# Moving the state-space output products one turn later, and fourteen matmuls on a tile of ones at the start

## The chip, the core and the metric

The kernel runs on one core of a Trainium2 chip. A core has a matmul engine (TensorE, "PE" in the profile, its weight loads "PEld"), a vector engine (VectorE, "DVE"), a scalar engine (ScalarE, "ACT"), a general engine (GpSimd, "POOL") and a queue that issues transfers (SyncE, "SP"). Each engine takes its instructions in the order of the program, and waits for others by semaphores. The metric is the time of one execution in microseconds of the device. Before the change it is 2964.65 us, the median of 3 runs (2963.62 to 2970.11).

## The reference

Two layers over 256 positions of width 4096. Layer 0 has a state-space mixer (S5), layer 1 a gated linear recurrence; both attend to a fixed memory. What matters here is the mixer of layer 0, cut from the reference:

```python
proj = rmsnorm(h, pre_norm[i]) @ w_in[i]
u, gate, q, q_gate = split(proj)                 # u: 3072 wide, 192 groups of 16 channels
ab = exp(lam * dt)                               # complex, 64 states to a group
x  = einsum('blgc,gpc->lbgp', u, bb)             # input products
s  = associative_scan(x with decay ab)           # complex states
y  = einsum(s_re, c_re) - einsum(s_im, c_im)     # output products
y  = y + d_skip * u
g  = gelu(y)
out = g * sigmoid(g @ w_glu + b_glu)
```

After it `out * silu(gate)` and the attention's part go through one output projection, and the normalised result is added to `h`.

## The kernel before

All matmuls with large weights run in *steps*. A step takes a block of 512 KB of weights (`raw`), which SP loads five steps ahead. ACT casts it to a rounded copy `hi` and DVE subtracts to get the rest `lo` (`split_w`, two steps ahead); TensorE then multiplies both parts (`mm_step`). There are three buffers for `raw` and six halves each for `hi` and `lo`, so the cast for step i + 2 waits for the matmuls of step i - 1, and the load for step i + 5 waits for the split of step i + 2.

The program is written out by `run`, one turn for each step: first what is due in that turn (`at(k, f)` puts a piece of work into turn k, and pieces of one turn run in the order in which they were put there), then the step's matmuls, the split of a later step, side work, and the load of a still later one. So the turn in which a piece stands sets its place in the queue of every engine that it uses.

The mixer is cut into 24 row groups `ct` of 128 channels. When the scan is done, `s5` gives each group a start turn S = S0 + 3·ct and puts its pieces into turns around it (`y_tasks`, lines 908 to 947):

- S - 9, S - 5, S - 2: SP loads the output coefficients as given (`s["craw"]`, tensor `in_s5c`), `b2` and `u`.
- S - 7: `y_coef`. POOL works out four sets of output coefficients, for the four positions of a block of time: per set two products over 128 x 128 (lines 883 and 884, into `P` and `Q`) and four sums over 64 x 64 (lines 887 and 888), 24 instructions in all. They go into `Cs[ct % 3]`: **three buffers in turn**, so group ct + 3 is written where group ct was.
- S: `d_mm`, 8 small matmuls into `psd`, which read sets 0 to 2 of that buffer.
- S + 1: `d_copy`, four copies by ACT from `psd` into `aux`.
- S + 2: `y_mm`, the output products. Three matmuls read `aux` and `u`, then 32 small ones read the states and the buffer `Cs[ct % 3]`, in the order set 1, set 2, set 3, set 0. All write one half of the PSUM tile `pm`.
- S + 3 to S + 8: skip term on DVE (`f3`), GELU on ACT and DVE, and the store of the result (`f8`, tensor `gF`).

While this runs, the steps are those of `gq0`, `q0` and the first of `k0`; at the same time the memory is normalised (`st` from `in_mem`) for `k0`. Three steps and one group's `d_mm` and `y_mm` make one period on TensorE.

At the very start SP loads the first weight block and the first parts of `x`; ACT makes the first operand `A` from them, and then TensorE has its first matmul.

Of the kernel before, what the change touches and what calls it, by code (L numbers as in the profile page):

```python
# [14 lines left out]
AF = mybir.ActivationFunctionType  # L15
# [13 lines left out]
L4 = 4  # L29
TQ = T // L4  # L30
MAGIC = 12582912.0

SM = {}
_o = 0
# [28 lines left out]
class Trunk:  # L63
# [77 lines left out]
    def at(self, k, fn):  # L141
        self.due.setdefault(max(k, self.step + self.late), deque()).append(fn)
# [6 lines left out]
    def setup(self):  # L149
        tc, ctx = self.tc, self.ctx  # L150
        P = lambda name, bufs, **kw: ctx.enter_context(tc.tile_pool(name=name, bufs=bufs, **kw))
        self.cpool = P("const", 1)
        self.wraw = P("wraw", 3)
        self.whi = P("whi", 6)
        self.wlo = P("wlo", 6)
        self.big = P("big", 1)
        self.ev = P("ev", 3)
        self.stp = P("st", 2)
        self.ps_acc = P("psacc", 4, space=PSUM)
        self.ps_x = P("psx", 3, space=PSUM)  # L160
        self.ps_m = P("psm", 1, space=PSUM)
        self.pm = self.ps_m.tile([128, 2, T], F32, name="pm")
        self.dram = P("dram", 1, space=DRAM)
        dt = lambda n, s, d=F32: self.dram.tile(s, d, name=n, tag=n)
        self.uF = dt("uF", [KE, 128, T])
        self.aD = dt("aD", [NT, 2, 2, 64])
        self.wD = dt("wD", [KE, 2, L4, 16, 512])
        self.uX = dt("uX", [KE, 2, L4, 64, 64])
        self.gF = dt("gF", [KE, 128, T])
        self.sil = dt("sil", [KE, 128, T])  # L170
        self.hs = dt("hs", [KE, 128, T])
        self.og = dt("og", [KD, 128, T])
        self.h1 = dt("h1", [KD, 128, T])
        self.qd = [dt(f"qd{i}", [KX, 128, T]) for i in range(2)]
        self.sq = [dt(f"sqd{i}", [KX, 128, T]) for i in range(2)]
        self.kd = [dt(f"kd{i}", [KX, 128, T]) for i in range(2)]
        self.vd = [dt(f"vd{i}", [2, 128, XA]) for i in range(2)]
        c = self.cpool
        self.sm = c.tile([128, SM_W], F32, name="sm")
        self.ones = c.tile([128, 128], F32, name="ones")  # L180
        self.ident = c.tile([128, 128], F32, name="ident")
        self.n4sp = c.tile([128, KE], F32, name="n4sp")
        self.acc = c.tile([128, 2, T], F32, name="acc")
        self.rbx = c.tile([128, T], F32, name="rbx")
        self.rbm = c.tile([128, T], F32, name="rbm")
        self.colm = c.tile([128, 2], F32, name="colm")
        self.nc.vector.memset(self.ones, 1.0)
        make_identity(self.nc, self.ident)

    def small(self, name, i, n=1):  # L190
        o = SM[name][0] + i
        return self.sm[:, o:o + n]
# [473 lines left out]
    def exp_gen(self, y, x, t):  # L666

        k, r, p, z, ki = t
        self.ts(y, x, -104.0, ALU.max, 88.0, ALU.min)
        self.ts(k, y, 1.4426950408889634, ALU.mult, MAGIC, ALU.add)  # L670
        self.ts(k, k, MAGIC, ALU.subtract)
        yield
# [19 lines left out]
    def sincos_gen(self, s, c, th, t):  # L692
        k, r, z, q, m1, m2 = t
        self.ts(k, th, 0.6366197723675814, ALU.mult, MAGIC, ALU.add)
        self.ts(k, k, MAGIC, ALU.subtract)
        yield
# [7 lines left out]
        self.ts(c, z, 2.443315711809948e-5, ALU.mult, -1.388731625493765e-3, ALU.add)  # L704
        self.ts(q, q, MAGIC, ALU.add)
        self.mul(s, s, z)
        self.mul(c, c, z)
        yield
        self.ts(q, q, MAGIC, ALU.subtract)
        self.ts(s, s, -1.6666654611e-1, ALU.add)  # L710
# [38 lines left out]
    def s5(self):  # L749
        I, at = self.I, self.at  # L750
# [112 lines left out]
        def y_load(ct, part):  # L863
            s = st.setdefault(ct, {})
            if part == 0:
                s["craw"] = v4(tail(1536 + 128 * (ct % 2), 128))
                self.dma(s["craw"], I["s5c"][ct])
            elif part == 1:
                s["b2"] = v4(tail(1792 + 256 * (ct % 2), 256))
                self.dma(s["b2"], I["s5b2"][ct])  # L870
            else:
                s["u"] = sp.tile([128, T], F32, name="u", tag="u")
                for i in range(4):
                    self.dma(s["u"][32 * i:32 * i + 32], self.uF[ct].rearrange("(q i) t -> i q t", i=4)[i])

        def y_coef(ct):
            s = st[ct]
            P, Q = v4(tail(2304, 128)), v4(tail(2432, 128))
            g = self.nc.gpsimd
            for i, (re, im) in enumerate(kc):  # L880
                C = Cs[ct % 3][:, i]
                b = lambda v: v[:, 4 * ct:4 * ct + 4].unsqueeze(1).unsqueeze(3).to_broadcast([128, 2, 4, 16])
                g.tensor_tensor(out=P, in0=s["craw"], in1=b(re), op=ALU.mult)
                g.tensor_tensor(out=Q, in0=s["craw"], in1=b(im), op=ALU.mult)
                for h in range(2):
                    r, c = slice(64 * h, 64 * h + 64), slice(16 * h, 16 * h + 16)
                    g.tensor_tensor(out=C[r, 0, :, c], in0=P[r, 0], in1=Q[r, 1], op=ALU.add)
                    g.tensor_tensor(out=C[r, 1, :, c], in0=Q[r, 0], in1=P[r, 1], op=ALU.subtract)

        def d_mm(ct):  # L890
            s = st[ct]
            s["d"] = self.ps_x.tile([128, 3, 32], F32, name="psd", tag="x")
            for k in range(2):
                for j in range(4):
                    self.mm(s["d"][32 * j:32 * j + 32], s["b2"][:, k, j, :], Cs[ct % 3][:, 0:3, k, j, :],
                            k == 0, k == 1, 66)

        def d_copy(ct):
            d = D[ct % 2]
            for j in range(4):  # L900
                r = slice(32 * j, 32 * j + 32)
                self.acopy(d[r, :, r], st[ct]["d"][r])

        def y_mm(ct):
            s = st[ct]
            ps = self.pm[:, 1, :].rearrange("p (e t) -> p e t", e=L4)
            s["y"] = ps
            C, d, u = Cs[ct % 3], D[ct % 2], s["u"].rearrange("p (e t) -> p e t", e=L4)
            for i in range(3):
                self.mm(ps[:, i:3, :], d[:, i, :], u[:, 0:3 - i, :], i == 0, False, 330 - 53 * i)  # L910
            for e in range(L4):
                o = e == L4 - 1
                for k in range(2):
                    for j in range(4):
                        self.mm(ps[32 * j:32 * j + 32, e, :], C[:, 0 if o else e + 1, k, j, :],
                                X[:, ct * 4 + j, k, o:o + TQ], o and k == 0, e > 1 and k == 1, 60)

        def y_tasks(ct, S):
            s = st.setdefault(ct, {})
            y = tail(256 * (ct % 4), 256)  # L920
            w = tail(1024 + 256 * (ct % 2), 256)

            def f3():
                self.stt(y.rearrange("p (t e) -> p e t", e=L4), s["u"].rearrange("p (e t) -> p e t", e=L4),
                         self.small("d", ct), s["y"], ALU.mult, ALU.add)

            def f4():
                self.act(w, y, AF.Square)
                self.act(w, w, AF.Identity, scale=0.044715, bias=self.ones[:, 0:1])

            def f8():
                self.dma(self.gF[ct], y)
                self.done.add(("g", ct))
                del st[ct]
            at(S - 9, lambda: y_load(ct, 0))
            at(S - 5, lambda: y_load(ct, 1))
            at(S - 7, lambda: y_coef(ct))
            at(S - 2, lambda: y_load(ct, 2))
            at(S, lambda: d_mm(ct))
            at(S + 1, lambda: d_copy(ct))  # L940
            at(S + 2, lambda: y_mm(ct))
            at(S + 3, f3)
            at(S + 4, f4)
            at(S + 5, lambda: self.mul(w, w, y))
            at(S + 6, lambda: self.act(w, w, AF.Sigmoid, scale=1.5957691216057308))
            at(S + 7, lambda: self.mul(y, y, w))
            at(S + 8, f8)

        a = z = 0
        last = -9  # L950
# [24 lines left out]
        S = self.step + 10  # L975
        for ct in range(KE):
            y_tasks(ct, S + 3 * ct)
# [440 lines left out]
```

## Time and profile before

| what | value |
|---|---|
| median of 3 runs | 2964.65 us |
| the profiled execution, its own time | 2964.16 us |
| its span in the profile | 2962.4 us |
| TensorE busy | 2894.9 us, 98% of the span |
| DVE, ACT, POOL busy | 1969.3, 1598.3, 303.7 us |
| from the first `d_mm` to the last | 643.61 to 917.73 us |
| POOL's coefficients, first start to last | 625.34 to 915.03 us |

A busy TensorE means that some matmul is under way, so idle time is what can be removed or added directly, and its clock is the other thing to look at: the profile has a column for the clock that was granted, 1.00 being the full 2.4 GHz and 0.50 the lower 1.2 GHz. In the stretch of the output products POOL is busy nearly all the time; elsewhere it has little to do.

### The profile page before, as it was taken

How to read it: one execution, taken by the hardware profiler on the slowest of the kernel's cores; microseconds unless marked ns; L12 is line 12 of the kernel's file. 1: busy time of each engine (PE TensorE's matmuls, PEld its weight loads, DVE VectorE, ACT ScalarE, POOL GpSimd, SP SyncE). 2: the span in 40 equal slices, each digit the busy share in tenths (PEclk: the TensorE clock that was granted, in tenths of full speed). 3: DMA queues.
4: the chain of work that ended last, by engine and by line, in shares of the span. 5: the costliest groups of instructions: out<-in, count | busy, mean ns of one | idle time of the engine just before them, and what ended most of it. 6: DMA issues, size and time to landing. Idle time of an engine off the chain costs nothing.

```text
span 2962.4 us, 53046 instructions
## 1 busy us (share of the span) xinstructions
PE 2894.9 (98%) x19182; PEld 2537.9 (86%) x19182; DVE 1969.3 (66%) x3559; ACT 1598.3 (54%) x3042; POOL 303.7 (10%) x607
## 2 busy tenths in 40 slices
PE   8989999999989999999999999999999999999996
PEld 8978888888879898888888888888888888888885
DVE  8776459976586556666555776578788766655555
ACT  6334554445465556566555564466666655555553
POOL 0000000059993000000000110000000000000001
PEclk9999999999999999999999999999999999999998
DMA  7688756665566676677666896666667575666664
GB/s 247 203 248 264 228 197 188 193 203 188 185 219 199 220 246 228 218 232 231 196 208 202 267 307 199 200 205 212 210 209 224 195 235 189 201 201 201 203 203 155
DMA packets 279319, 633.64 MB, mean 214 GB/s; under 512 B 42464, under 2 KB 149216, under 8 KB 279008
## 3 DMA queue, kind: packets, MB, share of 16 engines
q1 hardware_dynamic: 272848, 624.22, 66.5%
q0 software_dynamic: 4352, 4.20, 0.9%
q8 instruction: 150, 2.46, 0.3%
q10 hardware_dynamic: 1856, 1.84, 0.2%
q14 instruction: 113, 0.93, 0.1%
HBM read 585.47 MB, written 46.24 MB: 213 GB/s over the span
## 4 chain that ended last, share of the span: by engine, by line
PE 87%; DVE 5%; DMA 4%; issue 2%; ACT 1%; SPq 1%; POOL 0%; DVEq 0%; ACTq 0%
PE acc L131 83%; DVE lo L91 2%; PE pm L131 2%; DMA raw<-in_w_q 1%; PE psg L131 1%; DMA raw<-in_w_u 1%; DVE Bs L91 1%; PE psx L131 1%; ACT hi L127 1%; DVE e L91 1%; DMA st<-in_mem 1%; SPq L135 1%; DVE Bfin L91 0%; PE pso L131 0%; PE pss L131 0%
## 5 line engine op out<-in xcount | busy, mean ns | idle before, releaser
L91 DVE TENSOR_TENSOR lo<-raw,hi 128x512 fp32r<-128x512 f32 x1960 | 1315.6, 696 | 885.1 <-ACT hi L127 847.1
L127 ACT CAST hi<-raw 128x512 fp32r<-128x512 f32 x1960 | 1153.7, 619 | 818.1 <-PE acc L131 425.3
L131 PE MATMUL acc<-A,hi 128*128 128x512 f32 (+1 forms) x4768 | 1483.4, 370 | 22.0 <-ACT hi L127 13.7
L131 PE MATMUL acc<-A,lo 128*128 128x256 f32 x4160 | 1169.5, 281 | 4.6 <-DVE lo L91 4.4
L131 PEld LDWEIGHTS acc<-A,hi 128*128 128x128 f32 x4768 | 861.6, 190 | 185.0 <-ACT hi L127 16.5
L131 PEld LDWEIGHTS acc<-A,lo 128*128 128x128 f32 x4160 | 789.9, 190 | 11.4 <-DVE lo L91 10.3
L131 PE MATMUL acc<-Bhn,hi 128*128 128x512 f32 x2048 | 719.4, 396 | 3.3 <-ACT hi L127 3.3
L131 PE MATMUL acc<-Bhn,lo 128*128 128x256 f32 x2048 | 572.9, 280 | 1.3 <-DVE lo L91 1.3
L131 PEld LDWEIGHTS acc<-Bhn,hi 128*128 128x128 f32 x2048 | 384.8, 188 | 93.1 <-ACT hi L127 4.3
L131 PEld LDWEIGHTS acc<-Bhn,lo 128*128 128x128 f32 x2048 | 386.8, 189 | 2.9 <-DVE lo L91 2.6
L131 PE MATMUL acc<-Bmix,hi 128*128 128x512 f32 x1024 | 355.0, 394 | 0.0
L131 PE MATMUL acc<-Bmix,lo 128*128 128x256 f32 x1024 | 283.6, 277 | 0.0
L131 PEld LDWEIGHTS acc<-Bmix,hi 128*128 128x128 f32 x1024 | 192.0, 188 | 44.7
L131 PEld LDWEIGHTS acc<-Bmix,lo 128*128 128x128 f32 x1024 | 192.1, 188 | 0.0
L131 PE MATMUL acc<-hi,A 128*128 128x512 f32 x512 | 157.7, 389 | 0.0
L649 POOL TENSOR_TENSOR Bfin<-Bfin 128x1024 f32<-128x1024 f32 x4 | 10.3, 2586 | 1186.8 <-DVE Bfin L91 1186.8
L127 ACT COPY e<-acc 128x256 f32<-128x256 f32 x212 | 78.1, 368 | 90.2 <-PE acc L131 89.1
L131 PEld LDWEIGHTS acc<-hi,A 128*128 128x128 f32 x512 | 95.8, 188 | 19.7
L578 POOL DMA_DIRECT2D bh<-in_x x16 | 19.3, 1208 | 823.2 <-ACT hi L127 759.7
L123 ACT ACTIVATE e<-e 128x256 f32<-128x256 f32 x64 | 26.8, 418 | 139.7 <-DVE e L91 139.5
L131 PE MATMUL acc<-lo,A 128*128 128x512 f32 x256 | 99.6, 389 | 0.0
L91 DVE TENSOR_TENSOR e<-e,acc 128x256 f32<-128x256 f32 x212 | 84.4, 410 | 7.1 <-ACT e L127 7.1
(151 smaller groups left out, 1789.2 us busy)
## 6 DMA issues: line engine op xcount, KB each, us to landing
raw<-in_w_out SPq DMA_DIRECT2D x256, 512.0 KB, 4.2
raw<-in_w_u SPq DMA_DIRECT2D x192, 512.0 KB, 4.4
raw<-in_w_g SPq DMA_DIRECT2D x192, 512.0 KB, 4.0
raw<-in_w_glu SPq DMA_DIRECT2D x72, 512.0 KB, 4.2
raw<-in_w_gq SPq DMA_DIRECT2D x64, 512.0 KB, 4.4
raw<-in_w_q SPq DMA_DIRECT2D x64, 512.0 KB, 4.3
raw<-in_w_k SPq DMA_DIRECT2D x64, 512.0 KB, 4.5
raw<-in_w_v SPq DMA_DIRECT2D x64, 512.0 KB, 4.3
```

What stands on the lines that cost most here:

```text
L91: self.nc.vector.tensor_tensor(out=out, in0=a, in1=b, op=op)
L123: self.nc.scalar.activation(out=out, in_=a, func=f, **kw)
L127: self.nc.scalar.copy(out=out, in_=a)
L131: self.nc.tensor.matmul(out, lhsT=lhsT, rhs=rhs, start=start, stop=stop)
L135: self.nc.sync.dma_start(out=out, in_=in_)
L578: self.nc.gpsimd.dma_start(out=h, in_=self.I["x"][2 * c:2 * c + 2].rearrange("k p t -> p k t"), accum_op=ALU.add)
L649: self.nc.gpsimd.tensor_tensor(out=o, in0=o, in1=h, op=ALU.add)
```

## The change

```diff
+NWARM = 14
@@ setup
         make_identity(self.nc, self.ident)
+        for _ in range(NWARM):
+            self.nc.tensor.matmul(self.pm[:, 0, 0:128], lhsT=self.ones, rhs=self.ones, start=True, stop=True)
@@ y_tasks
             at(S, lambda: d_mm(ct))
             at(S + 1, lambda: d_copy(ct))
-            at(S + 2, lambda: y_mm(ct))
-            at(S + 3, f3)
-            at(S + 4, f4)
-            at(S + 5, lambda: self.mul(w, w, y))
-            at(S + 6, lambda: self.act(w, w, AF.Sigmoid, scale=1.5957691216057308))
-            at(S + 7, lambda: self.mul(y, y, w))
-            at(S + 8, f8)
+            at(S + 3, lambda: y_mm(ct))
+            at(S + 4, f3)
+            at(S + 5, f4)
+            at(S + 6, lambda: self.mul(w, w, y))
+            at(S + 7, lambda: self.act(w, w, AF.Sigmoid, scale=1.5957691216057308))
+            at(S + 8, lambda: self.mul(y, y, w))
+            at(S + 9, f8)
```

`y_mm` and all that follows it stand one turn later; the loads, `y_coef`, `d_mm` and `d_copy` stay. `y_mm(ct)` is now in the turn of `d_mm(ct + 1)` and ahead of it. `y_coef(ct + 3)` stands in turn S + 2 of group ct. It was behind `y_mm(ct)` in that turn; now it is one turn ahead of it, with the same buffer. So in the program's order the products of groups 0 to 20 read what `y_coef(ct + 3)` has written.

The first place is TensorE's queue at the first output products, group 0. `C_3035` is the first coefficient buffer, `Bs_370` the large tile with the states, and what stands in brackets are the engines or transfers that the row waits for. Before:

```order
L131 MATMUL acc<-A,lo 128x256
L131 MATMUL pm<-u,aux 128x192 [waits DMAHW6_49,DMAHW1_49,DMAHW7_49,DMAHW0_49,Activation_49]
L131 MATMUL pm<-u,aux 128x128
L131 MATMUL pm<-u,aux 128x64
L131 MATMUL pm<-Bs_370,C_3035 32x64 x16
L131 MATMUL pm<-Bs_370,C_3035 32x64 [waits Pool_49]
L131 MATMUL pm<-Bs_370,C_3035 32x64 x3
L131 MATMUL pm<-Bs_370,C_3035 32x64 [waits Pool_49]
L131 MATMUL pm<-Bs_370,C_3035 32x64 x11
L131 MATMUL acc<-A,hi 128x512
```

The two waits for POOL stand at set 3, the last that POOL writes for this group; sets 0 to 2 were already waited for by `d_mm`. The same place after the change (the lines of the file are one higher, and the buffers have other numbers: `C_3049` is the first coefficient buffer, `C_3050` the second):

```order
L132 MATMUL pm<-u,aux 128x64
L132 MATMUL pm<-Bs_384,C_3049 32x64 [waits Pool_49]
L132 MATMUL pm<-Bs_384,C_3049 32x64 x3
...
L132 MATMUL pm<-Bs_384,C_3049 32x64 [waits Pool_49]
L132 MATMUL pm<-Bs_384,C_3049 32x64 x11
L132 MATMUL psd<-C_3050,Bs_384 32x96 [waits DMAHW2_49]
```

Now each of the two halves (real and imaginary) of sets 1, 2 and 3 has a wait for POOL of its own, six in all, of which the first and the last are shown; `d_mm` of the next group, the row with `psd`, stands behind them and has none.

The second place is SP's queue in the middle of this stretch. `gF<-Bs` is the store of a finished group, `Bs<-in_s5c` the load of raw coefficients for a group six later. Before:

```order
L135 DMA raw<-in_w_q 128x1024
L135 DMA gF<-Bs_370 128x256
L135 DMA raw<-in_w_q 128x1024
L135 DMA Bs_370<-in_s5c 128x128
L135 DMA raw<-in_w_q 128x1024
L135 DMA u<-uF 32x256 x4
```

After:

```order
L136 DMA raw<-in_w_q 128x1024 x2
L136 DMA gF<-Bs_384 128x256
L136 DMA Bs_384<-in_s5c 128x128
L136 DMA raw<-in_w_q 128x1024
L136 DMA u<-uF 32x256 x4
```

The store went past one load of weights and now stands directly ahead of the load of raw coefficients. The queue of POOL is the same row for row before and after.

## Rows read from the trace of the kernel before

**Rows 1.** The page, part 1: busy time, share and instructions by engine.
```profile
PE 2894.9 (98%) x19182; PEld 2537.9 (86%) x19182; DVE 1969.3 (66%) x3559; ACT 1598.3 (54%) x3042; POOL 303.7 (10%) x607
```

**Rows 2.** Sum over the stretches of the 24 groups, 625.34 to 915.36.
```profile
sum 290.02, PE 279.48 PEld 243.66 DVE 195.27 ACT 165.88 POOL 269.44; mean PE 27.95 PEld 24.37 DVE 19.53 ACT 16.59 POOL 26.94
```

**Rows 3.** Waits of PE, 620 to 930: total us, times, longest.
```profile
PE pm L131 <- ACT aux L127: 10.5, 7, 3.3
```

**Rows 4.** Waits of ACT, 640 to 930, the largest.
```profile
ACT hi L127 <- DMA raw<-in_w_q: 44.8, 21, 5.7
```

**Rows 5.** Waits of SP's queue, 640 to 930, the largest.
```profile
SPq L135 <- POOL Bs L884: 113.3, 21, 7.3
```

**Rows 6.** Timeline of POOL: start us, length us, engine, line, instruction.
```profile
625.34 0.40 POOL L883 TENSOR_TENSOR Bs<-Bs,cf 128x128 f32<-128x128 f32 x1 [5.07 <-DMA Bs<-in_s5c]
...
651.63 0.40 POOL L883 TENSOR_TENSOR Bs<-Bs,cf 128x128 f32<-128x128 f32 x1
...
652.47 0.32 POOL L887 TENSOR_TENSOR Bs<-Bs 64x64 f32<-64x64 f32 x1
...
653.80 0.40 POOL L883 TENSOR_TENSOR Bs<-Bs,cf 128x128 f32<-128x128 f32 x1
...
656.78 0.40 POOL L883 TENSOR_TENSOR Bs<-Bs,cf 128x128 f32<-128x128 f32 x1
...
673.87 0.73 POOL L883 TENSOR_TENSOR Bs<-Bs,cf 128x128 f32<-128x128 f32 x1
...
915.03 0.33 POOL L888 TENSOR_TENSOR Bs<-Bs 64x64 f32<-64x64 f32 x1
```

**Rows 7.** Timeline of PE at the small matmuls of the mixer.
```profile
643.61 0.54 PE L131 MATMUL psd<-C,Bs 128*32 128x96 f32 x16
...
649.83 0.88 PE L131 MATMUL pm<-u,aux 128*128 128x192 f32 x6
650.64 1.11 PE L131 MATMUL pm<-Bs,C 128*32 128x64 f32 x64
...
654.70 0.54 PE L131 MATMUL psd<-C,Bs 128*32 128x96 f32 x16
...
772.57 0.98 PE L131 MATMUL pm<-u,aux 128*128 128x192 f32 x6 [0.83 <-ACT aux L127]
...
831.95 0.98 PE L131 MATMUL pm<-u,aux 128*128 128x192 f32 x6 [2.16 <-ACT aux L127]
...
917.73 0.54 PE L131 MATMUL psd<-Bs 128*32 128x96 f32 x16
```

**Rows 8.** Stretches: length, busy PE, PEld, DVE, ACT, POOL; clock, DMA, GB/s.
```profile
774.00:776.00 2.00, 2.00 (x52) 1.73 (x41) 2.00 (x4) 1.46 (x3) 1.92 (x4) 1.00 0.00 0
...
834.00:836.00 2.00, 2.00 (x25) 1.64 (x17) 0.93 (x3) 1.02 (x3) 1.86 (x5) 0.50 0.13 41
```

**Rows 9.** Transfers by kind: instructions, KB, median us to landing.
```profile
Bs<-in_s5c SPq DMA_DIRECT2D x24, 64.0 KB, 1.8
```

**Rows 10.** Timeline of the start.
```profile
0.84 0.17 DVE L187 MEMSET ones<- 128x128 f32 x1 [0.84 <-PEq L1400]
...
8.04 0.58 PE L131 MATMUL acc<-A,hi 128*128 128x256 f32 x1 [8.04 <-ACT A L123]
...
13.05 0.41 PE L131 MATMUL acc<-A,lo 128*128 128x256 f32 x1
...
13.69 0.41 PE L131 MATMUL acc<-A,lo 128*128 128x256 f32 x1
...
14.57 0.28 PE L131 MATMUL acc<-A,lo 128*128 128x256 f32 x1
...
14.93 0.28 PE L131 MATMUL acc<-A,lo 128*128 128x256 f32 x1
```

**Rows 11.** The start by stretch, columns as in Rows 8.
```profile
10.00:12.00 2.00, 2.00 (x12) 2.00 (x11) 2.00 (x5) 2.00 (x5) 0.00 (x0) 1.00 0.83 306
```

**Rows 12.** Matmuls on the tile of ones: ns min/median/max.
```profile
L131 PE MATMUL pm<-dg,ones x20: 270/275/580, 89.7 to 2940.4; 128*128 128x128 f32 x20
```

## The prediction

> **What bounds the kernel now.** I read the page's part 1 first: TensorE has work under way in 2894.9 us, 98% of the span [rows 1], so whatever moves TensorE's queue moves the end. Then I went to the stretch that the change touches, the 24 groups of output products, by stretches: from the first coefficient to the last POOL is busy 269.4 of 290.0 us, its gaps being those between its instructions, while TensorE with 279.5 still has idle time, and DVE with 195.3 and ACT with 165.9 are far from full [rows 2]. POOL's timeline gives its pace: group 0 starts at 625.34, group 4 at 673.87, and the last of group 23 ends at 915.03 + 0.33 = 915.36 [rows 6]; that is 241.5 us for the 20 groups from 4 on, 12.07 each. TensorE left alone needs less: from d_mm to d_mm, 643.61 to 654.70, are 11.09 us [rows 7]. In these, y_mm takes 649.83 to 650.64 + 1.11 = 651.75, that is 1.92, d_mm 0.54, and each of three steps (11.09 - 1.92 - 0.54) / 3 = 2.88. So POOL is the slower of the two, and TensorE ends the stretch on POOL's heels: its last d_mm starts at 917.73 [rows 7], 2.4 us behind POOL's last coefficient.
>
> The waits say how this shows. TensorE waits for `aux`, the copies, 10.5 us in 7 places [rows 3]. But the copies are late because ACT's queue stands at casts that wait 44.8 us for weights [rows 4], and the weights are late because SP's queue stands 113.3 us at the reload of raw coefficients, whose place POOL has not read yet [rows 5]. The end of that chain is POOL's pace.
>
> **The change, part by part.** *The turn between copy and product.* It takes away the reason that the trace names, up to 10.5 us. I count it at nothing: POOL runs through without a wait before, so a TensorE that comes sooner only meets it elsewhere.
>
> *The buffer.* This is what decides. Three buffers go in turn, and y_mm(ct) now stands behind y_coef(ct + 3), which writes its buffer; it reads what that wrote, and waits for it. Before, it needed POOL's group ct; now POOL must be three groups further.
>
> First stop: TensorE reaches y_mm(0) one step later than before, at 649.83 + 2.88 = 652.7. POOL's group 3 ended at 673.87 (the start of group 4) [rows 6]. While TensorE stands, the splits stop and DVE runs dry; POOL has a quicker pace when DVE leaves it alone: one set took 653.80 - 651.63 = 2.17 us, four make 8.7, against 12.07 on the mean [rows 6]. With two sets of group 2 left at 656.78, group 3 is complete at 656.78 + 2 x 2.17 + 8.7 = 669.8; I take 670. The ends are this and 673.9. TensorE stands about 17 us.
>
> The Trainium skill (SBUF — State Buffer, § Who interferes with whom) says that a DVE instruction with two SBUF inputs and a GpSimd instruction that reads SBUF exclude each other for a whole instruction; that is a mechanism for the two paces. By it the early end, 670, holds; without it the sum below would be 4 us larger. That the first set of group 2 took 2.17 us and the second 656.78 - 653.80 = 2.98 [rows 6] agrees with it.
>
> After that the two engines are tied. POOL's last write of group ct + 3 releases the rest of y_mm(ct): 12 of its 32 small matmuls, 12/32 of 1.11 us = 0.42; then d_mm(ct + 1), 0.54; only then may POOL write group ct + 4 where d_mm(ct + 1) has read. POOL meanwhile does the first two products, 652.47 - 651.63 = 0.84 us [rows 6, 7]. With some 0.2 us for each of the two signals (an estimate: y_mm's first small matmul follows its first three by less, but on one engine) TensorE's side is 1.36, so POOL loses about 0.5 us a group, 10 us over the 20 groups. Bounds: nothing, if the signals are quick, and 1.2 each, 24 us, if the raw coefficients come late too. They are loaded three turns before use, now behind a store that SP issues just ahead; SP gets there some 10 us into a period of 12.6, and the load lands in 1.8 [rows 9], so they just fit.
>
> POOL's own 12.07 a group I leave as they are: the same instructions beside the same DVE work. Then its last group ends at 670 + 241.5 + 10 = 921.5, against 915.36.
>
> The rest: before, TensorE had only d_mm(23) left to start at that point. Now it has y_mm(20)'s rest, and from d_mm(21) to d_mm(23) two periods. 921.5 + 0.2 + 0.42 + 2 x 11.09 = 944.3, against 917.73: **26.5 us later**. Both kernels have the same work behind that point, so nothing gives it back. All that follows y_mm, one turn later on DVE, ACT and SP, I put at nothing: these engines are covered by TensorE's standing.
>
> *The burst.* Fourteen matmuls of ones can start when DVE has written the tile, 0.84 + 0.17 = 1.01, and the first real matmul waits for ACT until 8.04 [rows 10]. That one's step has 24 matmuls. Three of them take 13.69 - 13.05 = 0.64 us, soon after 14.93 - 14.57 = 0.36 [rows 10]: if all ran at the second pace, 8 x 0.28 = 2.2 us are won. The stretch view gives a clock of 1.00 there [rows 11], so it doesn't show what the durations do. A matmul on ones leaves two records (20 for the ten of five norms) [rows 12]; at the slow pace, 0.64 / 3 each, 28 take 6.0 us and end at 7.0, before they are in the way; at 0.58 each, the longest in the row, they would end at 17.3 and cost 9.3 - 2.2 = 7. I take a gain of 1.8, by the nearer row, the pace of the first step.
>
> The Trainium skill (TensorE: Matmul & The Clock Gate, § Part 1) says that the throttled clock is the default and activity releases it. By it the burst wins up to the 2.2; by the granted clock in the row, 1.00, it would win nothing.
>
> **Sum.** The profiled execution took 2964.16 us, 0.5 below the median. 2964.16 + 26.5 - 1.8 = **2989 us**.
>
> **Rivals.** *The clock falls in every group* (12%). After a wait of 2.16 us the granted clock was 0.50 from 834 to 836; after 0.83 it stayed at 1.00 [rows 7, 8]. TensorE will stand 12.6 - 11.09 = 1.5 us per group, between these. The 2 us at half speed lose 1 us of work, which the standing covers; what costs is the tied part, 0.42 + 0.54, if it runs at half pace: 0.96 a group, 19 us over the 20, half of that if the clock falls in every second group. 2999 to 3008.
>
> *POOL makes up for it* (11%). If the signals hide fully (10 us less) and POOL is quicker beside a DVE that waits more often (3 us, a quarter microsecond in each of 12 groups), 2976. Against it: DVE's work per group is unchanged.
>
> *The wait never binds* (4%, the other side). If POOL is three groups ahead when y_mm comes, only the gains are left: 2964.2 - 10.5 - 1.8 = 2952. It decides at y_mm(0): group 3 would have to be done by 652.7, or 27.4 us after 625.34, 6.8 us for each of four groups, below POOL's quickest 8.7. The trace speaks against it.
>
> *Something behind it takes the loss up* (3%): 2964. TensorE's idle time behind this stretch is small, so I see no place.
>
> **How the numbers follow.** The forecast has 70%, within about 2979 to 2998 by the bounds on the first stop, the loop and the burst. The range is 2975 to 3010: it takes in the second rival and most of the first. A measurement of this kernel can tell about 0.2%, 6 us. Faster 0.04, within it 0.03, slower 0.93.
>
> **What would show it.** Right: TensorE's waits for `aux` are gone and its largest wait is for POOL at the products; the first is over 12 us and ends near 670; some 20 follow at 1 to 2 us; SP's wait for POOL shrinks; POOL's last coefficient is at about 921 and the last d_mm at about 944; nothing after it differs. The first step at the start takes about 3 instead of 5.1 us. Wrong: y_mm(0) starts near 653 without a wait, or the last d_mm is no later than 925, or waits for weights grow outside this stretch.

## The result and the profile after

The kernel after the change takes 3007.39 us (2995.87 to 3010.73, 4 runs), the kernel before 2964.28 (2963.62 to 2970.11, 4 runs): 1.0135 times as long, with an interval of 1.0121 to 1.015. The forecast was 2989, in a range of 2975 to 3010. The direction and the first part of the mechanism, the products that wait for POOL three groups further on, came as forecast; the loss is 43 us where 25 were forecast.

The profiled execution took 3009.41 us, with a span of 3007.6, so it lies 45.2 behind that of before. Part 1 of the page of the kernel after, beside [rows 1], shows that little work was added: TensorE has 28 instructions more, those of the burst. Of the 45.2 us TensorE is busy for 13.0, of which 4.8 are the burst and the rest the same matmuls at a lower clock for the most part (below); the other 32.2 are standing.

```profile
PE 2907.9 (97%) x19210; PEld 2550.1 (85%) x19210; DVE 1964.2 (65%) x3559; ACT 1599.8 (53%) x3042; POOL 289.4 (10%) x607
```

TensorE's waits in the kernel after, from 620 to 960, the largest two (total us, times, longest). Source lines have moved down, by one at the start of the program and by three in the mixer, so L890 is the first of POOL's sums, L887 before. `C` in a row is one of the first two coefficient buffers; the third lies in the large tile and is shown as `Bs`, as are POOL's two products.

```profile
PE pm L132 <- POOL C L890: 30.8, 15, 11.0
PE pm L132 <- POOL Bs L890: 14.0, 9, 2.3
```

The wait for `aux` [rows 3] is gone, and in its place stand 30.8 + 14.0 = 44.8 us for POOL's coefficients: the wait that the exchanged order of buffers was forecast to bring. POOL's own waits, 620 to 990, in the same columns, hold what the forecast lacked:

```profile
POOL Bs L886 <- DMA Bs<-in_s5c: 38.5, 13, 7.0
POOL C L890 <- PE psd L132: 2.3, 4, 0.6
POOL Bs L890 <- PE psd L132: 0.6, 1, 0.6
```

For the release by TensorE, to which the forecast gave 10 us, POOL waits 2.9. For the raw coefficients it waits 38.5, of which 5.09 is the first wait of the stretch, as before in [rows 6]; 33.4 us are new. SP's queue, 640 to 990:

```profile
SPq L136 <- DVE lo L92: 114.1, 60, 5.7
SPq L136 <- DVE Bs L105: 41.9, 14, 10.2
...
SPq L136 <- POOL Bs L887: 10.8, 2, 5.6
```

Before, SP stood 113.3 us at the raw coefficients and waited for POOL to have read their place [rows 5]. Now the place is read in time, and SP comes late to it, because it stands at weights whose buffers DVE has not yet read.

TensorE's timeline (start us, length us, instruction, in brackets the wait and its releaser): the first stop, a long group, and the last d_mm, whose start was 917.73 in [rows 7].

```profile
652.07 0.88 PE L132 MATMUL pm<-u,aux 128*128 128x192 f32 x6
663.99 0.72 PE L132 MATMUL pm<-Bs,C 128*32 128x64 f32 x16 [11.04 <-POOL C L890]
666.14 0.72 PE L132 MATMUL pm<-Bs,C 128*32 128x64 f32 x16 [1.43 <-POOL C L890]
668.29 1.15 PE L132 MATMUL pm<-Bs,C 128*32 128x64 f32 x32 [1.43 <-POOL C L890]
...
740.19 0.88 PE L132 MATMUL pm<-u,aux 128*128 128x192 f32 x6
741.00 0.43 PE L132 MATMUL pm<-Bs,C 128*32 128x64 f32 x16
743.07 0.60 PE L132 MATMUL pm<-Bs,C 128*32 128x64 f32 x16 [1.63 <-POOL C L890]
745.22 1.15 PE L132 MATMUL pm<-Bs,C 128*32 128x64 f32 x32 [1.55 <-POOL C L890]
746.14 0.87 PE L132 MATMUL psd<-C,Bs 128*32 128x96 f32 x16
...
757.45 0.88 PE L132 MATMUL pm<-u,aux 128*128 128x192 f32 x6
...
959.99 0.52 PE L132 MATMUL psd<-Bs 128*32 128x96 f32 x16
```

y_mm(0) starts at 652.07 (forecast 652.7) and stands on its small matmuls for POOL's second, third and fourth set of group 3 in turn: 11.04, 1.43 and 1.43, 13.9 us in all (forecast about 17). POOL's timeline gives the end of that group, the release, the last read of one place of raw coefficients, the longest late start, and the end of the stretch; these answer to [rows 6]:

```profile
668.60 0.40 POOL L886 TENSOR_TENSOR Bs<-Bs,cf 128x128 f32<-128x128 f32 x1
...
669.94 0.31 POOL L890 TENSOR_TENSOR C<-Bs 64x64 f32<-64x64 f32 x1 [0.59 <-PE psd L132]
...
743.73 0.40 POOL L887 TENSOR_TENSOR Bs<-Bs,cf 128x128 f32<-128x128 f32 x1
...
762.61 0.40 POOL L886 TENSOR_TENSOR Bs<-Bs,cf 128x128 f32<-128x128 f32 x1 [6.95 <-DMA Bs<-in_s5c]
...
935.09 0.50 POOL L891 TENSOR_TENSOR Bs<-Bs 64x64 f32<-64x64 f32 x1
```

Group 3 is done and group 4 starts at 668.60 (forecast 670), and the last coefficient ends at 935.59 (forecast 921.5). So the miss lies between these two: 267.0 us for 20 groups, 13.35 each, where 12.57 were forecast. The groups are uneven: the starts at 745.53, 762.61, 773.65 and 789.37 are 17.1, 11.0 and 15.7 us apart.

Why the group of 762.61 is late stands in SP's queue from the matmuls of 740 on:

```profile
739.78 0.38 SPq L136 DMA_DIRECT2D Bs<-in_s5c  x1
741.75 0.33 SPq L136 DMA_DIRECT2D raw<-in_w_q  x1
747.14 1.72 SPq L136 DMA_DIRECT2D u<-uF  x4
748.96 0.37 SPq L136 DMA_DIRECT2D Bs<-in_s5b  x1
753.38 4.09 SPq L136 DMA_DIRECT2D raw<-in_w_q  x2
757.52 1.23 SPq L136 DMA_DIRECT2D gF<-Bs  x1
758.84 0.38 SPq L136 DMA_DIRECT2D Bs<-in_s5c  x1
```

POOL last read the place at 743.73 + 0.40 = 744.1. SP issues the load into it at 758.84, 14.7 us later, since it works through its list: 5.1 us without an issue ahead of `u`, 4.1 ahead of the two weights and some 3 more between them, then a store. The load then takes longer than the 1.8 us of [rows 9] (the transfers of 640 to 940 by kind, instructions, KB, median us to landing):

```profile
Bs<-in_s5c SPq DMA_DIRECT2D x21, 64.0 KB, 3.5
```

The long groups also have a low clock. The stretches around the two waits of 1.63 and 1.55 us (length, busy PE, PEld, DVE, ACT, POOL, granted clock, DMA share, GB/s):

```profile
742.00:744.00 2.00, 0.60 (x16) 0.32 (x16) 0.00 (x0) 0.00 (x0) 1.81 (x6) 1.00 0.89 293
...
746.00:748.00 2.00, 2.00 (x35) 1.63 (x28) 0.67 (x1) 0.89 (x4) 1.35 (x5) 0.50 0.00 0
```

From 746 on TensorE is busy throughout, and runs at 0.50, the lower level, to 750; from 750 to 752 the granted clock is 0.63 on the mean, then 1.00 again. d_mm stands at 746.14 and the next y_mm at 757.45, so the three steps take 757.45 - 746.14 - 0.87 = 10.4 us against 8.6 (three times 2.88) in the forecast. Over the stretch from the first to the last d_mm the same matmuls keep TensorE busy for 270.6 us, 7.0 more than before (263.6), at a granted clock of 0.92 on the mean against 0.98.

At the start of the program (TensorE's timeline of the kernel after) the burst ends before the first real matmul, and that runs at the quick pace:

```profile
1.06 4.77 PE L191 MATMUL pm<-ones 128*128 128x128 f32 x28 [1.06 <-DVE ones L188]
8.09 0.91 PE L132 MATMUL acc<-A,hi 128*128 128x256 f32 x2 [2.26 <-ACT A L124]
8.83 0.28 PE L132 MATMUL acc<-A,lo 128*128 128x256 f32 x1
...
9.19 0.28 PE L132 MATMUL acc<-A,lo 128*128 128x256 f32 x1
...
102.81 0.47 PE L132 MATMUL acc<-A,hi 128*128 128x256 f32 x2 [0.57 <-ACT hi L128]
...
210.60 0.80 PE L132 MATMUL acc<-A,hi 128*128 128x512 f32 x1 [5.76 <-ACT hi L128]
```

From 8.83 on a group of three takes 9.19 - 8.83 = 0.36 us, where it took 0.64 before [rows 10].

### The profile page after: what moved, and what is told of

Its sections match the earlier page's. It is cut to its first block, busy times and chain, and to the rows that moved or that the text cites. A ratio compares the mean times of both kernels' runs of the same rounds, so it can differ in the third digit from the quotient of the medians.

```text
span 3007.6 us, 53075 instructions
## 1 busy us (share of the span) xinstructions
PE 2907.9 (97%) x19210; PEld 2550.1 (85%) x19210; DVE 1964.2 (65%) x3559; ACT 1599.8 (53%) x3042; POOL 289.4 (10%) x607
## 4 chain that ended last, share of the span: by engine, by line
PE 85%; POOL 5%; DVE 3%; DMA 3%; issue 2%; ACT 1%; SPq 1%; ACTq 0%; DVEq 0%; POOLq 0%
PE acc L132 81%; POOL C L890 1%; DVE lo L92 1%; POOL C L891 1%; DMA Bs<-in_s5c 1%; PE psg L132 1%; POOL Bs L887 1%; PE pm L132 1%; PE psx L132 1%; POOL Bs L886 1%; DVE Bs L92 1%; ACT hi L128 1%; DMA raw<-in_w_u 1%; SPq L136 1%; DMA raw<-in_w_g 1%
```

## The experiments

The theory: the loss is the exchanged order of the coefficients and the products in one buffer, in two parts. POOL must be three groups further when TensorE multiplies, and the raw coefficients come late. Rivals: the low clock of the long groups, the loads of `u`, the burst. Each run is compared with runs of the kernel before on the same chip.

**The order of the buffer restored.** In the kernel after, POOL's coefficients are issued one turn later, so that they stand behind the products again.

```diff
-            at(S - 7, lambda: y_coef(ct))
+            at(S - 6, lambda: y_coef(ct))
```

> The change with y_coef one turn later as well (S - 6), so that in the program's order the coefficients of group ct + 3 are again written behind the products of group ct. Theory of the buffer: TensorE no longer needs POOL three groups ahead, the loss goes, 2955 to 2972, d_mm(23) at 912 to 922. Rival, the turn itself (stores ahead of the load of raw coefficients, loads of u close behind f3): at least half of the loss stays, 2985 or more.

Measured: 2963.62 us against 2966.0, ratio 0.9994 (0.9985 to 1.0004). The whole loss is gone. The wait of SP's queue, 640 to 930, is that of [rows 5] again:

```profile
SPq L136 <- POOL Bs L887: 109.0, 21, 7.7
```

The waits of TensorE for `aux` stay gone but for 0.4 us in one place, and yet nothing is gained that can be told: POOL runs through and bounds the stretch, as the first step of the forecast had it. This run also gives the raw coefficients one turn more between load and use; the next one doesn't.

**A fourth buffer.** The order stays as in the kernel after, but the buffer of y_mm(ct) is no longer the one that y_coef(ct + 3) writes.

```diff
-        Cb = [sp.tile([128, 1024], F32, name=f"C{i}", tag=f"C{i}", bufs=1) for i in range(2)] + [tail(2560, 1024)]
+        Cb = [sp.tile([128, 1024], F32, name=f"C{i}", tag=f"C{i}", bufs=1) for i in range(3)] + [tail(2560, 1024)]
...
-                s["u"] = sp.tile([128, T], F32, name="u", tag="u")
+                s["u"] = tail(3584, 256) if ct % 2 else sp.tile([128, T], F32, name="u", tag="u", bufs=1)
...
-                C = Cs[ct % 3][:, i]
+                C = Cs[ct % 4][:, i]
...
```

> The change with four coefficient buffers in place of three (one of the two u tiles moved into the large tile to make room), so the products of group ct read what was written for ct although y_coef(ct + 3) stands ahead of them. Theory of the buffer: 2955 to 2972, and no wait of the products for POOL of over 3 us. Rival, the turn itself: 2985 or more.

Measured: 2961.74 us against 2966.0, ratio 0.9987 (0.9978 to 0.9997). The one turn costs nothing by itself; the shared buffer costs all of it.

**Raw coefficients with three places, loaded three turns earlier.**

```diff
-                s["craw"] = v4(tail(1536 + 128 * (ct % 2), 128))
+                s["craw"] = v4(tail((1536, 1664, 3584)[ct % 3], 128))
...
-            at(S - 9, lambda: y_load(ct, 0))
+            at(S - 12, lambda: y_load(ct, 0))
```

> The change with three places for the raw coefficients and their load three turns earlier (S - 12); the buffer order stays as in the change, so the products of groups 0 to 20 read the coefficients of ct + 3. Theory of the late load: POOL's waits for in_s5c (38.5 us in 13 places) go but for the first, the loop falls from 13.35 us a group to 12.1 to 12.6, and the time to 2984 to 2994, the size of the forecast. Rival, the lower clock after long waits makes the long groups and the load is only late with them: POOL waits for psd instead, 3000 or more.

Measured: 2982.59 us against 2966.0, ratio 1.006 (1.0045 to 1.0075). POOL's wait for the load is the one at the start alone, and its release by TensorE costs 2.5 us (POOL's waits, 620 to 1000):

```profile
POOL Bs L886 <- DMA Bs<-in_s5c: 5.1, 1, 5.1
POOL Bs L890 <- PE psd L132: 1.9, 1, 1.9
POOL C L890 <- PE psd L132: 0.6, 1, 0.6
```

The clock is 1.00 over a stretch in which the kernel after has 0.92 to 1.00 by 50 us (the stretch row, columns as above):

```profile
700.00:850.00 150.00, 140.75 (x1719) 120.40 (x1708) 90.63 (x145) 80.48 (x188) 138.84 (x306) 1.00 0.65 187
```

So 16.6 us of loss are left without the late load, a little less than was expected, and about 26 of the 43 came with it.

**The load one turn earlier, in the same two places.** This asks whether the place or the turn in SP's queue made it late.

```diff
-            at(S - 9, lambda: y_load(ct, 0))
+            at(S - 10, lambda: y_load(ct, 0))
```

> The change with the raw coefficients loaded one turn earlier (S - 10) into the same two places; buffer order as in the change (the products of groups 0 to 20 read the coefficients of ct + 3). If the load is late by its turn in SP's queue, and not for want of a place, the short waits of POOL (0.5 to 3 us) go and the long ones (4 to 7 us) shrink by a step of 2.9: POOL's waits for in_s5c fall from 38.5 to below 18 us, the time to 2984 to 2997. If the place is what holds it, SP waits for POOL instead and the time stays at 3000 or more.

Measured: 2984.47 us against 2965.9, ratio 1.0063 (1.0044 to 1.0083). One turn is enough. POOL's largest wait of this kernel, 620 to 1000, is nearly all the first load:

```profile
POOL Bs L886 <- DMA Bs<-in_s5c: 5.6, 2, 5.3
```

So the load was late by its turn in the list, not for want of a place. Its landing still takes 3.5 us by the median, and no longer matters. TensorE's timeline of this kernel shows what a group now looks like:

```profile
726.07 0.82 PE L132 MATMUL pm<-Bs 128*32 128x64 f32 x32 [1.34 <-POOL Bs L890]
...
737.88 0.82 PE L132 MATMUL pm<-Bs,C 128*32 128x64 f32 x32 [0.83 <-POOL C L890]
```

From 700 to 800 the nine groups have one wait each, 0.41 to 1.34 us, where a long group of the change has two of 1.6, and the granted clock is 1.00 from 700 to 850.

**Three places for `u`.** SP also waits 41.9 us for DVE's f3, which frees the place of `u` and now comes one turn later.

```diff
-                s["u"] = sp.tile([128, T], F32, name="u", tag="u")
+                s["u"] = sp.tile([128, T], F32, name="u", tag="u", bufs=3)
```

> The change with three u tiles instead of two, so that the load of u in turn S + 4 no longer waits for f3 of the same turn; buffer order as in the change (the products of groups 0 to 20 read the coefficients of ct + 3). If SP's standing at the loads of u (41.9 us in the changed kernel) is what makes the raw coefficients late, POOL's waits for in_s5c fall below 15 us and the time to 2984 to 2995. If SP stands at the weights whose split waits for TensorE's steps, the loads of weights behind take over the wait and the time stays at 3000 to 3012.

Measured: 3003.06 us against 2966.12, ratio 1.0128 (1.0112 to 1.0144), no better than the change. That wait vanishes, and SP stands at the next things in its list (147.0 us at the weights that DVE has to read, where it was 114.1). POOL still waits 35.9 us for raw coefficients. The loads of `u` are not the cause.

**The burst alone and the change without it.**

```diff
-NWARM = 14
+NWARM = 0
```

> The change without the fourteen matmuls on ones. In the trace of the changed kernel the burst put the state-space stretch 0.6 us earlier (first d_mm at 643.02 against 643.61), the rest of what it won at the start (2.5 us at 102.8) was given back at a wait that ends at 210.6. So 3008, within a few us of the changed kernel. If the burst did harm further on, this one is faster than 3000.

Measured: 3012.11 us against 2966.0, ratio 1.0156 (1.0138 to 1.0174), an interval that overlaps that of the change, so no harm of the burst further on shows. The kernel before with the burst added:

```diff
+        for _ in range(NWARM):
+            self.nc.tensor.matmul(self.pm[:, 0, 0:128], lhsT=self.ones, rhs=self.ones, start=True, stop=True)
```

> The kernel before with the fourteen matmuls on ones and nothing else. By the trace of the changed kernel the first step is 2.2 to 2.5 us shorter and most of it is lost again at the wait that ends near 210, so 2962 to 2965, no difference that can be told. If what the start wins were kept, 2961.5 to 2962.5.

Measured: 2967.40 us against 2966.12, ratio 1.0004 (0.9994 to 1.0013): no difference that these runs can tell. (Both medians lie a little above the 2962 to 2965 that was expected.)

**The exchange without the moved products.** In the kernel before, POOL's coefficients are issued one turn earlier, ahead of y_mm in its old place.

```diff
-            at(S - 7, lambda: y_coef(ct))
+            at(S - 8, lambda: y_coef(ct))
```

> The kernel before with one edit: y_coef one turn earlier (S - 8), so that it stands ahead of the products of group ct - 3 with the same buffer, while the products stay in their turn S + 2; the products of groups 0 to 20 read the coefficients of ct + 3, as in the change. Theory of the buffer: six waits for POOL in each y_mm, a first stop that ends near 670, and a loss of the order of the change's, 2980 to 3010. If it is the turn of the products that costs, 2960 to 2970.

Measured: 3075.52 us against 2966.12, ratio 1.0368 (1.0353 to 1.0384), far above what was expected. POOL's waits of this kernel, 620 to 1000:

```profile
POOL Bs L883 <- DMA Bs<-in_s5c: 41.2, 20, 5.4
POOL C L887 <- PE psd L131: 38.6, 12, 5.0
POOL Bs L887 <- PE psd L131: 22.4, 7, 4.8
```

and a group in TensorE's timeline:

```profile
731.54 1.15 PE L131 MATMUL pm<-Bs,C 128*32 128x64 f32 x32 [1.55 <-POOL C L887]
737.94 0.54 PE L131 MATMUL psd<-Bs 128*32 128x96 f32 x16
```

What I had not reckoned with: here d_mm(ct + 1), which releases POOL's next buffer, does not follow y_mm(ct) at once but a whole step later, 731.54 + 1.15 to 737.94, 5.2 us, with a granted clock of 0.50 from 732 to 736, where such a step took 2.88 before. POOL stands for that step, 61 us in all. In the change the two are neighbours, and the same release costs 0.59 us where it is waited for at all. The raw coefficients, which here have only one turn between load and use, are late about as much as in the change, by 36 us besides the first wait of 5. So the exchange has a second price, and whether it is paid depends on what stands between the last reader and the release.

**A quarter of POOL's work on DVE.** If POOL's pace bounds the stretch, less work there must gain. In the kernel before, with the burst, DVE computes the fourth set of each group (`y_coef3`, the same six instructions on DVE, whose code is not shown).

```diff
-            for i, (re, im) in enumerate(kc):
+            for i, (re, im) in enumerate(kc[:3]):
...
+            at(S - 4, lambda: y_coef3(ct))
```

> The kernel before with the burst, and with the fourth set of coefficients (set 3) worked out by DVE in turn S - 4 instead of POOL, 6 instructions of some 0.2 to 0.3 us a group. If POOL's pace bounds the stretch in the kernel before, POOL needs some 9 us a group, less than TensorE's 11.09, and d_mm(23) comes at 898 to 906 instead of 917.7: 2945 to 2955. If DVE, at 65% with 6 more instructions a group, or the memory's normalisation bounds it, no gain: 2960 or more.

Measured: 2951.23 us against 2966.12, ratio 0.995 (0.9936 to 0.9965). POOL now waits for TensorE; its largest wait from 620 to 1000:

```profile
POOL C L890 <- PE pm L132: 21.3, 11, 2.6
```

**The same with the products one turn later.** The moved lines are those of the change, with the coefficients one turn later too, so that no order in a buffer is exchanged. The lines shown are against the kernel before; the burst and the code of DVE's set are as in the run above.

```diff
-            at(S - 9, lambda: y_load(ct, 0))
+            at(S - 8, lambda: y_load(ct, 0))
...
-            at(S - 7, lambda: y_coef(ct))
+            at(S - 6, lambda: y_coef(ct))
+            at(S - 3, lambda: y_coef3(ct))
...
-            at(S + 2, lambda: y_mm(ct))
+            at(S + 3, lambda: y_mm(ct))
```

> The kernel with burst and with set 3 on DVE, and with the products one turn later as in the change, but with y_coef, the raw coefficients and DVE's set one turn later too, so that the buffer order holds. With POOL no longer the bound, the turn between copy and product can take away the remaining waits for aux (4.8 us in 4 places): 2945 to 2951. If POOL or DVE is the bound again, 2950 to 2955.

Measured: 2944.67 us against 2965.9, ratio 0.9935 (0.9915 to 0.9955). It has the lowest median of the study, and is faster than the kernels before and after. Its interval overlaps that of the run before it, so a gain of the turn by itself isn't shown; by the profiles the stretch from the first to the last d_mm is 257.1 us (638.80 to 895.91) against 261.5 (638.12 to 899.65), and TensorE's waits for `aux` are 1.2 us in one place against 4.8 in four.

## Why the prediction was right, and where its size was off

The time lies in the stated range, but above the 2979 to 2998 that the main forecast was given. The upper part of the range was there for the rival of the falling clock, and the loss that filled it came by another way, with the late raw coefficients. That the range holds the time is in part luck.

**The bound** was read rightly. POOL's pace held the stretch: without the waits for `aux` hardly anything is gained, and with a quarter of POOL's work gone 15 us are.

**The turn** costs nothing, as forecast, and gains little if anything: with the order restored no difference can be told, and with four buffers (both with the burst) the time is 4 us shorter, with an interval of the ratio that ends just below 1.

**The buffer** decides, as forecast. All of the loss goes with either run that undoes it.

**The first stop** came within 2 us: begun at 652.07, group 3 complete and group 4 begun at 668.60. POOL ran its quick pace, 659.99 to 668.60, 8.6 us for four sets, where the working had 8.7, and DVE stood for nearly all of the stop:

```profile
669.51 0.67 DVE L105 SCALAR_TENSOR_TENSOR Bs<-u,sm,pm 128x256 f32<-128x256 f32 x1 [14.74 <-PE pm L132]
```

The Trainium skill (SBUF — State Buffer, § Who interferes with whom) gave the early end, and the trace agrees with that end (670) and not with the 673.9 of an unchanged pace.

**The loop** is the term that was mis-sized. "So they just fit" was the failing step: SP was to get to the raw coefficients some 10 us into a period of 12.6 and their landing was put at 1.8 us, from a kernel in which SP waits at exactly that load and so finds the rest of its list done. The working also counts three turns between this load and its use, while the program has two (S - 9 and S - 7). In the change SP hardly waits there any more, its list is behind, and the load went out 14.7 us after the release in the group shown and lands in 3.5 by the median. The sum by the trace, against the forecast: group 4 starts 1.4 earlier; 20 groups take 267.0 instead of 251.5, +15.5; from POOL's end to the last d_mm there are 959.99 - 935.59 = 24.4 instead of 22.8, +1.6. Together 15.7, which is 959.99 - 944.3. Inside the 20 groups the two sizes were wrong in opposite ways: the waits for raw coefficients are 33.4 (forecast nothing, with 24 us as the upper bound of all, 1.2 a group, which no row gave), those for the release 2.9 (forecast 10), and POOL's own pace without waits is (267.0 - 33.4 - 2.9) / 20 = 11.5 us instead of 12.07. DVE is busy for 56% of the stretch instead of 67%, which fits with a quicker POOL but isn't shown to be the reason. The 0.2 us for a signal came from no row either: POOL's sum that ends at 744.85 + 0.32 = 745.17 releases the matmul of 745.22, 0.05 us later.

With the load in time, the stretch from the first to the last d_mm is 294.8 us (640.54 to 935.29, in the run with the load one turn earlier) against 274.1 before (643.61 to 917.73) and 317.0 after (643.02 to 959.99). So of its 42.9 us of loss 20.6 stay when the load is in time, and the rest, 22.2, came with the late load. The 20.6 are what the order of the buffer costs by itself. Where they come up can be read from that run: against before and from the first d_mm on, group 4 starts 4.6 us earlier on POOL, the 20 groups from there take 244.5 instead of 241.5, and from POOL's last coefficient to the last d_mm there are 24.6 us instead of 2.4, since TensorE, three groups behind, has that much left to do.

**Nothing behind gives it back**: 42.3 us at the last d_mm are 45.2 at the last load of w_out (2920.3 before, 2965.5 after). The 2.9 between are no more than executions differ by: from the last d_mm to the end of the span there are 2044.7 us before and 2047.6 after, and 2045.7 to 2048.8 in the profiles of the other runs, the longest in the kernel before with the burst alone. The medians are 43 apart.

**The burst** did what it was forecast to do at the start, and no gain at the end can be told. The quick pace at the first step won 2.5 us by the wait at 102.81, which stood at 105.30 before; at 210.60 TensorE waits 5.76 us for the same cast for which it waited 3.94 before, and starts 0.2 us earlier than then. By the profile that cast follows a piece of DVE, which begins at 208.01 after 8.1 us of waiting for a load (`aD`); before, it followed its own load of weights. In the run with the burst alone the same wait ends at 206.48, so this is not what becomes of the gain each time. The term of -1.8 is not borne out: with the burst alone the median is 1.3 us longer, with an interval from -1.8 to +3.9. The Trainium skill (TensorE: Matmul & The Clock Gate, § Part 1), by which the burst was to win the first step, agrees with the 0.36 us there. The granted clock of 1.00 in [rows 11] did not show the slow pace of before.

**The rival of the falling clock** had its time in the right place (2999 to 3008) and half of its reason. The clock fell to 0.50 in the long group shown and lengthened its three steps by about 1.8 us. That it also delays DVE's splits and with them SP is likely, but not shown. But with the load one turn earlier TensorE still waits for POOL once a group, and the clock stays at 1.00 from 700 to 850, where the change has 0.95; from 850 to 900 it falls there too, to 0.93 on the mean against 0.86. So in the groups from 700 to 850 the fall came with the late loads. TensorE is busy for 270.6 us of the change's stretch and for 262.5 of that run's, with the same matmuls: 8.1 of the 22.2 us are slower matmuls, the other 14.1 more standing. Whether the loads would be late without the lower clock was not tried apart, so how much of the standing goes back to it stays open. **POOL makes up for it** holds for its two reasons, quick signals and a quicker POOL, and was outweighed. **The wait never binds** and **something behind takes it up** did not occur.

## What to carry to other kernels

Before work in a ring of buffers is moved by a turn, write down for each buffer the order of writer and reader in the program, since a move past the writer of the next round turns a free buffer into a wait of a whole ring, here three groups of POOL and 20.6 us. Then ask for each queue that the stalled engine had been holding back: a load that was early because its queue stood waiting at it can become late once the queue waits elsewhere, and the old trace shows neither its turn nor its landing. And a wait by which one engine shows up is no gain if another engine's pace sets the stretch: here the 10 us of waits were worth nothing, and a quarter less work on that other engine 15.

## What the runs showed of the hardware

Two waits of 1.63 and 1.55 us, with 0.60 us of small matmuls between them, were followed by a granted clock of 0.50, and so were 1.88 and 1.55 at 771 to 773. One wait a group of up to 1.34 us, from 700 to 800 in the kernel with the load one turn earlier, left the clock at 1.00, and after the single wait of 2.26 us behind the burst the matmuls ran at the quick pace. But the length of the waits alone doesn't decide it. In the kernel after, a single wait of 2.15 us and a pair of 1.24 and 1.55 left the granted clock at 1.00 (690 to 700 and 800 to 850):

```profile
694.30 0.83 PE L132 MATMUL pm<-Bs 128*32 128x64 f32 x32 [2.15 <-POOL Bs L890]
...
800.71 0.83 PE L132 MATMUL pm<-Bs,C 128*32 128x64 f32 x32 [1.55 <-POOL C L890]
```

In the kernel before, a single one of 2.16 was followed by 0.50 [rows 7, 8]. The forecast had taken one wait of 1.5 us a group as the case to weigh; in the long group shown two came in a row.

At the start the granted clock doesn't tell the pace. In [rows 10, 11] a group of three matmuls takes 0.64 us at a granted clock of 1.00; in the run of the exchange without the moved products such a group also takes 0.64 (733.21 to 733.85), there at a granted clock of 0.50, and 0.36 at 1.00 (739.10 to 739.46).

The same 64 KB load took 1.8 us to land where SP had stood waiting at it, and 3.5 us in the change, where SP issues it right behind other transfers (medians of 21 each, 640 to 940). That those are the reason was not tried apart.
